# The mLSTM states of a bidirectional mixer block: value index innermost, and one instruction per step in place of scans over time

## The chip, the cores and the metric

The kernel runs on one core of one Trainium2 chip. The time is the device time of one launch in microseconds, the median of several runs. TensorE's clock shows in the profile as a granted share of its full speed.

## What is computed

A backbone of two layers (DEPTH = 2) works on 1280 tokens: 256 context tokens and 1024 latent ones, 1024 features each. A layer normalizes, projects its input into the columns of four mixers (mLSTM, differential attention, gated linear attention GLA, gated DeltaNet), runs the four, and joins them in one output projection with a gated residual. The second layer returns only latent tokens. The change concerns the mLSTM, which runs in both directions over the tokens; the backward direction takes the context tokens from last to first, then the latent ones from last to first.

```python
def _mlstm_run(q, k, v, log_i, log_f, state):
    ...
    def step(carry, inp):
        C, n, m = carry
        ...
        num = (w_inter[..., None] * jnp.einsum('bhtd,bhde->bhte', qc, C)
               + jnp.einsum('bhts,bhse->bhte', s, vc))
        nq = w_inter * jnp.einsum('bhtd,bhd->bht', qc, n) + jnp.sum(s, axis=-1)
        h = num / jnp.maximum(jnp.abs(nq), jnp.exp(-m_t))[..., None]
        ...
        C = w_c[..., None, None] * C + jnp.einsum('bhs,bhsd,bhse->bhde', w_s, kc, vc)
        n = w_c[..., None] * n + jnp.einsum('bhs,bhsd->bhd', w_s, kc)
        return (C, n, m_new), h
    state, h = lax.scan(step, state, tuple(_to_chunks(a) for a in (q, k, v, log_i, log_f)))
```

The memory C (64 by 64 for each of four heads) and its normalizer n (64) thus follow a recurrence over chunks of tokens: the new one is the old one times a decay, plus the chunk's own product of keys and values. The kernel keeps n as a 65th column of C.

## The kernel before

**Tiles and names.** The 1280 tokens are NT = 10 tiles of 128 (2 context, 8 latent), and a tile is the mLSTM's chunk. The states lie in two tiles of on-chip memory, cs0 (forward, d = 0) and cs1 (backward, d = 1). Axis 0 of cs holds two heads (x) of 64 key features each, axis 1 the pair of heads (hp), then come 130 values (2 times 65; of these, 65 belong to each x) and innermost the 10 places in the order of the direction (p). Two values that are neighbours in one state therefore lie ten elements apart. wdec holds the decay of each tile, direction and head, one number for each of the 128 lanes.

**The state part** (`mlstm`, before the mark "mlstm.out") goes through all ten tiles in both layers. `state_in` loads the tile's keys (kq, three buffers) and values (mv), TensorE transposes the keys into a PSUM tile m, an evacuation (`evac`, a copy that goes to ScalarE or VectorE) brings them to a buffer named pd (three buffers), and GpSimd weighs the values beside them. `state_out` forms the products of keys and weighed values in another PSUM tile m and copies them to cs at place p, 64 lanes by 130 values at a time: four copies a tile, two for each direction, none for a direction's last tile. After the ten tiles come eight scans over time (the instruction TENSOR_TENSOR_SCAN, 64 lanes by 65 values by 10 places), each of which turns the products of one head and direction into states. A scan needs a tile of decays as large as its own operand. It is built in a pd buffer by two GpSimd memsets and by copies from wdec, four times a layer.

**The output part** (`first`, `second`, `post`, `norms`) goes over the layer's output tiles, ten in layer 0 and eight in layer 1. `load` fetches for each tile a pd buffer with a broadcast of rs_NG (128 by 1024, 0.52 MB), kq (128 by 1024), mv, and two wb; GpSimd and ScalarE form the weights, TensorE multiplies (pp from kq; m from cs and wb, which is where cs is read; m from mv and pd), VectorE normalizes, and SyncE writes the tile's result from hy to y in the chip's memory. pd, kq and wb have three buffers each, so a tile's load waits until the tile three before it is done.

**What runs beside it.** `out_first` takes the output product of the other three mixers' finished features (k = 2, 3, 6, 7) tile by tile: y is loaded and turned (tr, yT), TensorE forms o, VectorE multiplies by the gate (o from o and gtb) and adds the residual (st from o and st), and SyncE writes st to xp in the chip's memory and loads the next residual into st (two buffers). Only when this is through for all tiles ("out first") can `outproj` begin, which does the remaining k (0, 1, 4, 5): it loads y, x from xp and the gate gtb, turns, multiplies, and adds. In layer 1 GLA's results are also still being written (y from hy, four transfers at a time, and gz loads).

**What sets the order.** Each part is a strand with a rank. A scheduler that runs when the kernel is built takes instructions from the strands by estimated clocks of the engines and puts each at the end of its engine's queue. All instructions go through one helper line, L406, so the profile's rows are told apart by the names of tiles. An engine's queue is worked off in order. SyncE's (SP) holds nearly all transfers: if one waits for its data or its buffer, all behind it wait too. A change of one strand's instructions moves those of every strand behind it.

Of the kernel before, what the change touches and what calls it, by code (L numbers as in the profile page):

```python
# [17 lines left out]
ALU = mybir.AluOpType  # L18
# [8 lines left out]
NT = T // 128  # L27
NCT = NCTX // 128
# [8 lines left out]
ORDER = (tuple(range(NT)), tuple(range(NCT - 1, -1, -1)) + tuple(range(NT - 1, NCT - 1, -1)))  # L37
# [392 lines left out]
def _build(tc, nc, A, out, root, dbg):  # L430
    q_ = Issue()
    q_.log = dbg.get("log")
    V, S, G, P = (Eng(q_, e, r) for e, r in zip("VSGP", (nc.vector, nc.scalar, nc.gpsimd, nc.tensor)))
# [1425 lines left out]
    def mlstm_open(L, st):  # L1859
        M = Box()  # L1860
        M.p = p = Pool(st, "ml")
        M.ps = Pool(st, "mlps", PSUM)

        M.cs = [p([128, 2, 130, NT], f"cs{d}") for d in range(2)]

        M.vt = [p([128, 4, 65], f"mv{i}") for i in range(3)]
        M.wdec = p([128, 2, 2, NT], "wdec")
        return M

    def mlstm(L, M):  # L1870
        l = L.l
        mp_, pps, cs, wdec = M.p, M.ps, M.cs, M.wdec
# [40 lines left out]
        def state_out(t, kt, vws):  # L1913
            pu = pps([128, 2, 2, 65], "m", 2)
            for d, vw in vws.items():
                for h in range(4):
                    hp, x = divmod(h, 2)
                    P.matmul(pu[64 * x:64 * x + 64, d, hp, :], kt[:, 64 * h:64 * h + 64], vw[:, h, :],
                             start=True, stop=True, tile_position=(0, 64 * x))
            for d in vws:  # L1920
                p = ORDER[d].index(t)
                for x in range(2):
                    xs = slice(64 * x, 64 * x + 64)
                    evac(cs[d][xs, :, 65 * x:65 * x + 65, p], pu[xs, d])
        prev = None
        for t in range(NT):
            cur = state_in(t)
# [1 line left out]
                state_out(*prev)  # L1929
            prev = cur  # L1930
        state_out(*prev)
        for d in range(2):
            for hp in range(2):
                dec = mp_([128, 1024], "pd", 3)[:, :650].rearrange("p (a b) -> p a b", b=NT)
                if d == 0:
                    sl = [(wdec[:, 0, hp, 1:NT - 1], 1, NT - 1)]
                else:
                    sl = [(wdec[:, 1, hp, 0:1], 1, 2), (wdec[:, 1, hp, NT - 1:NCT:-1], 2, NT - 1)]

                G.memset(dec[:, :, 0:1], 0.0)  # L1940
                G.memset(dec[:, :, NT - 1:NT], 0.0)
                for (src, a, b) in sl:
                    V.tensor_copy(dec[:, :, a:b], src.unsqueeze(1).to_broadcast([128, 65, b - a]))
                for x in range(2):
                    xs = slice(64 * x, 64 * x + 64)
                    c_ = cs[d][xs, hp, 65 * x:65 * x + 65, :].rearrange("p a b -> p (a b)")
                    V.tensor_tensor_scan(c_, dec[xs].rearrange("p a b -> p (a b)"), c_, 0.0, ALU.mult, ALU.add)
        mark(f"{l}mlstm.out")
        for b in ("mo", "mz"):
            q_.need((l, b))  # L1950
# [38 lines left out]
        def post(i):  # L1989
            b = lds[i]  # L1990
            t = b.t
# [4 lines left out]
            for d in range(2):  # L1996
                p = ORDER[d].index(t)
                nv = pps([128, 4, 65], "m", 2)
                nvs.append(nv)
                if p > 0:  # L2000
                    for hp in range(2):
                        P.matmul(nv[:, 2 * hp:2 * hp + 2, :].rearrange("p a b -> p (a b)"), b.wb[:, d, hp, :], cs[d][:, hp, :, p - 1],
                                 start=(hp == 0), stop=False)
                for h in range(4):
                    P.matmul(nv[:, h, :], b.pd[:, d, h, :], b.vt[:, h, :], start=(p == 0), stop=(p == 0 or h == 3))
# [935 lines left out]
```

## Time and profile before

| | |
|---|---|
| median of 3 runs | 2445.36 us (2436.24 to 2446.64) |
| the profiled execution | 2444.86 us |
| its span, first to last instruction | 2443.0 us |
| mean granted TensorE clock | 0.937 |
| TensorE busy | 2141.1 us, 88% of the span |
| VectorE busy | 1513.1 us, 62% |
| ScalarE busy | 987.4 us, 40% |
| GpSimd busy | 850.4 us, 35% |
| DMA | 335.37 MB, mean 137 GB/s |

Read the shares as averages over a launch whose parts have different limits. Layer 0's state part and output part of the mLSTM lie between about 1045 and 1250 us of the span, layer 1's between about 2190 and 2396 us. PE is TensorE's multiplications, PEld its weight loads, DVE is VectorE, ACT ScalarE, POOL GpSimd, SP SyncE; an arrow reads output, then input.

### The profile page before, as it was taken

How to read it: one execution, taken by the hardware profiler on the slowest of the kernel's cores; microseconds unless marked ns; L12 is line 12 of the kernel's file. 1: busy time of each engine (PE TensorE's matmuls, PEld its weight loads, DVE VectorE, ACT ScalarE, POOL GpSimd, SP SyncE). 2: the span in 40 equal slices, each digit the busy share in tenths (PEclk: the TensorE clock that was granted, in tenths of full speed). 3: DMA queues.
4: the chain of work that ended last, by engine and by line, in shares of the span. 5: the costliest groups of instructions: out<-in, count | busy, mean ns of one | idle time of the engine just before them, and what ended most of it. 6: DMA issues, size and time to landing. Idle time of an engine off the chain costs nothing.

```text
span 2443.0 us, 57689 instructions
## 1 busy us (share of the span) xinstructions
PE 2141.1 (88%) x23367; PEld 1762.3 (72%) x23367; DVE 1513.1 (62%) x2676; ACT 987.4 (40%) x2169; POOL 850.4 (35%) x1075
## 2 busy tenths in 40 slices
PE   5899999999898998886868798889999989977888
PEld 1656778888776687865756677888888667866776
DVE  3586679555386854546556396686642778555665
ACT  2346412333376853222424255412322677533240
POOL 1343523554122225241522163623442122254340
PEclk8899999999999999988989899999999999976989
DMA  7347643455513134157953135432444331353694
GB/s 260 116 133 228 198 140 109 138 152 157 143 46 91 51 84 147 51 143 213 279 178 133 43 124 173 158 113 93 148 149 126 91 100 38 75 152 85 186 277 172
DMA packets 348051, 335.37 MB, mean 137 GB/s; under 512 B 93146, under 2 KB 292282, under 8 KB 347274
## 3 DMA queue, kind: packets, MB, share of 16 engines
q1 hardware_dynamic: 347786, 331.69, 45.6%
q8 instruction: 185, 3.03, 0.5%
q14 instruction: 80, 0.66, 0.1%
HBM read 226.78 MB, written 107.43 MB: 137 GB/s over the span
## 4 chain that ended last, share of the span: by engine, by line
PE 55%; DMA 13%; DVE 11%; issue 8%; ACT 6%; SPq 5%; POOL 2%; ACTq 0%; POOLq 0%; DVEq 0%
PE mm L406 26%; PE po L406 5%; SPq L406 5%; PE tr L406 4%; PE o L406 4%; PE sc L406 3%; PE p L406 3%; PE pd L406 3%; DVE st L406 2%; DMA wm<-in_w_mod 2%; PE puw L406 2%; ACT p L406 2%; PE m L406 2%; DVE cacc L406 1%; DMA KT<-akh 1%
## 5 line engine op out<-in xcount | busy, mean ns | idle before, releaser
L406 PE MATMUL mm<-w,hT 128*128 128x256 f32 x4512 | 645.6, 294 | 20.7 <-DVE st L406 10.0
L406 PEld LDWEIGHTS mm<-w,hT 128*128 128x128 f32 x4512 | 580.9, 195 | 52.9 <-issue 20.4
L406 PE MATMUL mm<-hT,w 128*128 128x512 f32 (+1 forms) x1680 | 388.9, 377 | 19.0 <-DVE w L406 4.9
L406 PEld LDWEIGHTS mm<-hT,w 128*128 128x128 f32 x1680 | 283.1, 195 | 90.0 <-issue 19.6
L406 DVE TENSOR_REDUCE st<-sc 128x1 f32<-128x1024 f32 (+1 forms) x200 | 200.2, 1027 | 69.8 <-PE sc L406 68.3
L406 ACT ACTIVATE p<-sc,st 128x256 f32<-128x256 f32 (+1 forms) x272 | 211.3, 786 | 68.8 <-DVE st L406 54.8
L406 POOL TENSOR_TENSOR w<-wr,w 128x512 fp32r<-128x512 f32 x62 | 87.4, 1411 | 235.5 <-ACT w L406 199.4
L406 POOL TENSOR_TENSOR hss<-hss,mhalf 128x2 f32<-128x2 f32 (+2 forms) x72 | 105.7, 1467 | 181.7 <-DVE hss L406 175.8
L406 PE MATMUL o<-wo,yT 128*128 128x512 f32 x540 | 155.2, 425 | 8.6 <-DVE x L406 7.1
L406 PE MATMUL sc<-KT,qt 96*128 96x512 f32 (+1 forms) x400 | 124.9, 402 | 30.3 <-DMA KT<-akh 13.3
L406 POOL TENSOR_TENSOR ss<-ss,mhalf 128x1 f32<-128x1 f32 (+1 forms) x39 | 68.2, 1749 | 193.4 <-DVE ss L406 185.4
L406 PEld LDWEIGHTS o<-wo,yT 128*128 128x128 f32 x540 | 105.7, 202 | 34.7 <-issue 5.6
L406 ACT COPY st<-mm 128x512 f32<-128x512 f32 (+1 forms) x83 | 45.8, 552 | 202.0 <-PE mm L406 140.9
L406 ACT COPY wt<-tr 128x512 f32<-128x512 f32 (+1 forms) x200 | 102.2, 511 | 60.4 <-PE tr L406 59.8
L406 PE MATMUL o<-w,yT 128*128 128x512 f32 x324 | 107.3, 462 | 21.8 <-DVE st L406 12.3
L406 PE MATMUL tr<-k_ident,p 128*128 128x128 f32 x656 | 114.7, 280 | 7.5 <-ACT wt L406 7.2
L406 POOL TENSOR_TENSOR st<-st 128x1 f32<-128x1 f32 (+1 forms) x136 | 26.6, 195 | 266.5 <-ACT p L406 196.9
L406 ACT CAST w<-wr 128x512 fp32r<-128x512 f32 x128 | 76.8, 620 | 103.7 <-PE mm L406 52.6
L406 PEld LDWEIGHTS sc<-KT,qt 96*128 96x128 f32 x400 | 63.8, 197 | 60.4 <-ACT p L406 32.0
L406 PE MATMUL po<-wt,av 128*64 128x128 f32 x1312 | 103.0, 282 | 2.0 <-DVE aacc L406 2.0
L406 DVE SCALAR_TENSOR_TENSOR p<-p,st,p 128x1280 f32<-128x1280 f32 (+1 forms) x72 | 103.0, 1431 | 2.6 <-POOL st L406 2.5
L406 DVE TENSOR_TENSOR w<-wr,w 128x512 fp32r<-128x512 f32 x66 | 59.1, 895 | 68.6 <-ACT w L406 64.9
(315 smaller groups left out, 4125.8 us busy)
## 6 DMA issues: line engine op xcount, KB each, us to landing
wr<-in_w_in SPq DMA_DIRECT2D x64, 512.0 KB
wm<-in_w_mod SPq DMA_DIRECT2D x64, 256.0 KB
y<-y SPq DMA_DIRECT2D x36, 256.0 KB
xp<-st SPq DMA_DIRECT2D x18, 512.0 KB
pd<-rs_NG SPq DMA_DIRECT2D x18, 512.0 KB
kq<-kq SPq DMA_DIRECT2D x18, 512.0 KB
x<-xp SPq DMA_DIRECT2D x18, 512.0 KB
wm<-in_w_mod SPq DMA_DIRECT2D x16, 512.0 KB
```

What stands on the lines that cost most here:

```text
L406: r = fn(*a, **k)
```

## The change

cs is laid out with the value index innermost, so that one state of one pair of heads is 130 neighbouring elements. The scans go, and with them the memsets and copies that built the decays in pd buffers. For the forward direction each tile's state is made in `state_out` itself: four VectorE instructions a tile (64 lanes by 65 values; tiles after the first) take the previous state, multiply it by the decay, one number per lane, and add the product straight from PSUM; these replace two copies. For the backward direction the copies stay, and after all tiles 16 VectorE instructions a layer (128 lanes by 130 values) go from state to state in the backward order. The multiplication that reads cs now reads neighbouring elements.

```diff
-        M.cs = [p([128, 2, 130, NT], f"cs{d}") for d in range(2)]
+        M.cs = [p([128, 2, NT, 130], f"cs{d}") for d in range(2)]
...
-                    xs = slice(64 * x, 64 * x + 64)
-                    evac(cs[d][xs, :, 65 * x:65 * x + 65, p], pu[xs, d])
+                    xs, es = slice(64 * x, 64 * x + 64), slice(65 * x, 65 * x + 65)
+                    if d == 1 or p == 0:
+                        evac(cs[d][xs, :, p, es], pu[xs, d])
+                    else:
+                        for hp in range(2):
+                            V.scalar_tensor_tensor(cs[d][xs, hp, p, es], cs[d][xs, hp, p - 1, es], wdec[xs, d, hp, t:t + 1],
+                                                   pu[xs, d, hp, :], ALU.mult, ALU.add)
...
-        for d in range(2):
+
+        for p in range(1, NT - 1):
+            t = ORDER[1][p]
             for hp in range(2):
-                dec = mp_([128, 1024], "pd", 3)[:, :650].rearrange("p (a b) -> p a b", b=NT)
-                if d == 0:
-                    sl = [(wdec[:, 0, hp, 1:NT - 1], 1, NT - 1)]
-                else:
-                    sl = [(wdec[:, 1, hp, 0:1], 1, 2), (wdec[:, 1, hp, NT - 1:NCT:-1], 2, NT - 1)]
-
-                G.memset(dec[:, :, 0:1], 0.0)
-                G.memset(dec[:, :, NT - 1:NT], 0.0)
-                for (src, a, b) in sl:
-                    V.tensor_copy(dec[:, :, a:b], src.unsqueeze(1).to_broadcast([128, 65, b - a]))
-                for x in range(2):
-                    xs = slice(64 * x, 64 * x + 64)
-                    c_ = cs[d][xs, hp, 65 * x:65 * x + 65, :].rearrange("p a b -> p (a b)")
-                    V.tensor_tensor_scan(c_, dec[xs].rearrange("p a b -> p (a b)"), c_, 0.0, ALU.mult, ALU.add)
+                V.scalar_tensor_tensor(cs[1][:, hp, p, :], cs[1][:, hp, p - 1, :], wdec[:, 1, hp, t:t + 1], cs[1][:, hp, p, :],
+                                       ALU.mult, ALU.add)
...
-                        P.matmul(nv[:, 2 * hp:2 * hp + 2, :].rearrange("p a b -> p (a b)"), b.wb[:, d, hp, :], cs[d][:, hp, :, p - 1],
+                        P.matmul(nv[:, 2 * hp:2 * hp + 2, :].rearrange("p a b -> p (a b)"), b.wb[:, d, hp, :], cs[d][:, hp, p - 1, :],
```

The scheduler then places all later instructions anew. Three places show it. Numbers behind a name are buffers.

**First place, the end of layer 0's state part.** This is VectorE's queue of the kernel before, from the first tile of decays (pd_13801) to the sum whose result st_13602 SyncE then writes to xp; cs_2116 is forward, cs_2117 backward, and the scans print as SCALAR_TENSOR_TENSOR of 64x650 from pd and cs.

```order
L406 COPY pd_13801<-wdec_12923 128x65x8
L406 SCALAR_TENSOR_TENSOR cs_2116_12918<-pd_13801,cs_2116_12918 64x650 x2
L406 SCALAR_TENSOR_TENSOR wo_2237_13758<-wr_13753,wcol_13580,wo_2235_13756 128x512
L406 COPY pd_13823<-wdec_12923 128x65x8
L406 TENSOR_TENSOR yT_2244_13817<-tr_13818,yT_2243_13816 128x512
L406 SCALAR_TENSOR_TENSOR cs_2116_12918<-pd_13823,cs_2116_12918 64x650
L406 TENSOR_TENSOR o_13764<-o_13764,gtb_13653 128x512
L406 SCALAR_TENSOR_TENSOR cs_2116_12918<-pd_13823,cs_2116_12918 64x650
L406 SCALAR_TENSOR_TENSOR wo_2250_13839<-wr_13835,wcol_13580,wo_2248_13837 128x512
L406 COPY pd_13853<-wdec_12923 128x65
L406 COPY pd_13853<-wdec_12923 128x65x7
L406 TENSOR_TENSOR st_13602<-o_13764,st_13602 128x512
```

The four forward scans stand ahead of that sum; the four backward ones follow behind it, among further sums of `out_first`.

The same place on VectorE's queue in the changed kernel, from the copy of tile 9's transposed keys (pd_13766) on:

```order
L406 COPY pd_13766<-m_13763 128x256
L406 SCALAR_TENSOR_TENSOR wo_2229_13728<-wr_13724,wcol_13570,wo_2227_13726 128x512
L406 SCALAR_TENSOR_TENSOR wo_2230_13729<-wr_13724,wcol_13570,wo_2228_13727 128x512
L406 SCALAR_TENSOR_TENSOR cs_2116_12918<-cs_2116_12918,wdec_12923,m_13774 64x65 x4
L406 TENSOR_TENSOR o_13735<-o_13735,gtb_13639 128x512
L406 TENSOR_TENSOR st_13582<-o_13735,st_13582 128x512
L406 SCALAR_TENSOR_TENSOR cs_2116_12918<-cs_2116_12918,wdec_12923,m_13815 64x65 x4
L406 COPY cs_2117_12919<-m_13815 64x2x65 x2
L406 TENSOR_TENSOR yT_2246_13811<-tr_13812,yT_2245_13810 128x512
L406 SCALAR_TENSOR_TENSOR wo_2239_13789<-wr_13785,wcol_13570,wo_2237_13787 128x512
L406 SCALAR_TENSOR_TENSOR cs_2117_12919<-cs_2117_12919,wdec_12923 128x130 x15
L406 SCALAR_TENSOR_TENSOR wo_2240_13790<-wr_13785,wcol_13570,wo_2238_13788 128x512
```

No scan stands here any more: four forward steps follow each tile's products, and the sum st_13582 of `out_first` stands between tile 8's and tile 9's. The backward steps follow as one row of 15 and one of 1.

SyncE's queue of the kernel before at this place, from the last tile's keys (kq_13698) to the first load of the output part (pd_13894):

```order
L406 DMA kq_13698<-kq_43_120 128x2x128
L406 DMA mv_2118_12920<-mv_71_148 128x4x64
L406 DMA wr_13703<-in_w_out 128x1024
L406 DMA xp_47_124<-st_13320 128x1024
L406 DMA wr_13753<-in_w_out 128x1024
L406 DMA st_13744<-in_x 128x1024
L406 DMA y_13814<-y_31_108 128x2x256
L406 DMA wr_13835<-in_w_out 128x1024
L406 DMA xp_47_124<-st_13602 128x1024
L406 DMA st_13864<-in_x 128x1024
L406 DMA y_13888<-y_31_108 128x2x256
L406 DMA pd_13894<-rs_NG_196 128x8x128
```

The last keys stand ahead of the write of st_13320 to xp, and the first output load stands behind the write of st_13602.

SyncE's queue of the changed kernel, between the same two:

```order
L406 DMA xp_47_124<-st_13320 128x1024
L406 DMA wr_13724<-in_w_out 128x1024
L406 DMA st_13715<-in_x 128x1024
L406 DMA kq_13760<-kq_43_120 128x2x128
L406 DMA mv_2118_12920<-mv_71_148 128x4x64
L406 DMA wr_13785<-in_w_out 128x1024
L406 DMA y_13808<-y_31_108 128x2x256
L406 DMA xp_47_124<-st_13582 128x1024
L406 DMA st_13834<-in_x 128x1024
L406 DMA pd_13893<-rs_NG_196 128x8x128
```

The last keys (kq_13760) now stand behind the write of st_13320 and a load of st; the first output load (pd_13893) still stands behind the second write, now of st_13582.

**Second place, the end of layer 0's output part.** This is SyncE's queue of the kernel before, from the write of the last of the mLSTM's results (hy_14753) to the first loads for `outproj` (y, x, gtb); wr and kq_44 belong to the next layer's projection.

```order
L406 DMA y_31_108<-hy_14753 128x256
L406 DMA wr_14774<-in_w_in 128x4x256
L406 DMA wr_14779<-in_w_in 128x4x256
L406 DMA kq_44_121<-in_k_zero 64x2x1280
L406 DMA y_14785<-y_31_108 128x2x256
L406 DMA x_14786<-xp_47_124 128x1024
L406 DMA kq_44_121<-in_k_zero 64x2x1280
L406 DMA wr_14825<-in_w_in 128x4x256
L406 DMA wr_14827<-in_w_in 128x4x256
L406 DMA y_14848<-y_31_108 128x2x256
L406 DMA x_14849<-xp_47_124 128x1024
L406 DMA gtb_14855<-gt_19_96 128x1024
```

The write of the last result (hy_14753) stands first, and x and gtb, on which `outproj`'s first sums wait, behind it.

The changed kernel's SyncE queue at this place, with hy_14814 the last result:

```order
L406 DMA y_31_108<-hy_14640 128x256
L406 DMA oz_14657<-oz_45_122 128x512
L406 DMA y_14663<-y_31_108 128x2x256
L406 DMA x_14664<-xp_47_124 128x1024
L406 DMA y_31_108<-hy_14724 128x256
L406 DMA oz_14746<-oz_45_122 128x512
L406 DMA x_14770<-xp_47_124 128x1024
L406 DMA gtb_14772<-gt_19_96 128x1024
L406 DMA y_31_108<-hy_14776 128x256
L406 DMA y_14804<-y_31_108 128x2x256
L406 DMA y_31_108<-hy_14814 128x256
```

The first y and x for `outproj` stand ahead of the last three results, the second x and gtb ahead of the last two.

**Third place, the start of layer 1's output part.** This is SyncE's queue of the kernel before; the transfers y from hy in groups of four and the gz loads are GLA's, and pd_27093 is the first load of the mLSTM's output part.

```order
L406 DMA xp_48_125<-st_26313 128x1024
L406 DMA st_26828<-x_26_103 128x1024
L406 DMA y_27020<-y_32_109 128x2x256
L406 DMA y_32_109<-hy_26938 32x8x64 x4
L406 DMA gz_27041<-gz_90_167 32x8x64 x4
L406 DMA xp_48_125<-st_26519 128x1024
L406 DMA y_27087<-y_32_109 128x2x256
L406 DMA pd_27093<-rs_NG_206 128x8x128
L406 DMA kq_27096<-kq_44_121 128x8x128
L406 DMA mv_4110_25326<-mv_72_149 128x4x64
L406 DMA wb_27099<-rs_WI_207 64x4x128 x2
L406 DMA oz_27094<-oz_46_123 128x512
```

Three writes to xp and a group of GLA's writes stand here, the first pd load behind them all.

The changed kernel's SyncE queue at this place:

```order
L406 DMA xp_48_125<-st_26338 128x1024
L406 DMA pd_26955<-rs_NG_206 128x8x128
L406 DMA kq_26958<-kq_44_121 128x8x128
L406 DMA mv_4097_25245<-mv_72_149 128x4x64
L406 DMA wb_26961<-rs_WI_207 64x4x128 x2
L406 DMA oz_26956<-oz_46_123 128x512
L406 DMA oz_26972<-oz_46_123 128x512
L406 DMA st_26913<-x_26_103 128x1024
L406 DMA y_32_109<-hy_26965 32x8x64 x4
L406 DMA gz_27015<-gz_90_167 32x8x64 x4
L406 DMA pd_27058<-rs_NG_206 128x8x128
```

The first pd load stands right behind the write of st_26338, which answers to st_26313 of before, and the second (pd_27058) behind the next group of GLA's writes; later writes to xp stand behind both.

## Rows read from the trace of the kernel before

**Rows 1.** page, section 1: busy time of each engine, share of the span, instructions

```profile
PE 2141.1 (88%) x23367; PEld 1762.3 (72%) x23367; DVE 1513.1 (62%) x2676; ACT 987.4 (40%) x2169; POOL 850.4 (35%) x1075
```

**Rows 2.** windows of layer 0: stretch, its us, busy (x) of PE PEld DVE ACT POOL, PEclk, DMA share, GB/s

```profile
1070.00:1090.00 20.00, 19.73 (x382) 15.68 (x381) 6.14 (x12) 4.21 (x10) 7.03 (x9) 0.87 0.53 143
...
1130.00:1150.00 20.00, 12.98 (x44) 10.01 (x45) 15.95 (x22) 3.04 (x9) 1.97 (x3) 0.67 0.68 199
...
1150.00:1170.00 20.00, 17.00 (x93) 14.38 (x91) 8.96 (x21) 7.03 (x26) 7.80 (x11) 0.91 1.09 273
...
1170.00:1200.00 30.00, 26.67 (x148) 24.23 (x148) 18.95 (x42) 11.71 (x41) 15.40 (x21) 0.89 1.07 282
```

**Rows 3.** timeline of VectorE, layer 0: start us, us, operation

```profile
1123.91 3.03 DVE L406 TENSOR_TENSOR_SCAN cs<-pd,cs 64x650 f32<-64x650 f32 x2
...
1133.31 0.68 DVE L406 TENSOR_TENSOR st<-o,st 128x512 f32<-128x512 f32 x1
...
1138.62 3.01 DVE L406 TENSOR_TENSOR_SCAN cs<-pd,cs 64x650 f32<-64x650 f32 x2
```

**Rows 4.** SyncE's DMA issues, layer 0, same columns: start us, us, transfer

```profile
1106.36 0.55 SPq L406 DMA_DIRECT2D kq<-kq  x1
...
1113.69 0.33 SPq L406 DMA_DIRECT2D xp<-st  x1
...
1118.51 0.33 SPq L406 DMA_DIRECT2D st<-in_x  x1
...
1134.01 0.33 SPq L406 DMA_DIRECT2D xp<-st  x1
...
1137.60 0.59 SPq L406 DMA_DIRECT2D pd<-rs_NG  x1
```

**Rows 5.** timeline of TensorE, layer 0

```profile
1110.15 0.66 PE L406 MATMUL m<-k_ident,kq 128*128 128x128 f32 x2 [3.65 <-DMA kq<-kq]
```

**Rows 6.** tile cs, whole span: count, duration ns min/median/max, first and last start us

```profile
L406 PE MATMUL m<-cs,wb x136: 389/412/586, 1151.8 to 2388.0; 128*128 128x130 f32 x136
...
L406 DVE COPY cs<-m x32: 375/392/410, 1078.9 to 2279.8; 64x130 f32<-64x130 f32 x32
...
L406 DVE TENSOR_TENSOR_SCAN cs<-pd,cs x16: 1491/1506/1818, 1123.9 to 2301.8; 64x650 f32<-64x650 f32 x16
```

**Rows 7.** tile wdec on VectorE, same columns

```profile
L406 DVE COPY pd<-wdec x12: 214/394/439, 1123.4 to 2296.9; 128x520 f32<-128x520 f32 x4, 128x65 f32<-128x65 f32 x4, 128x455 f32<-128x455 f32 x4
```

**Rows 8.** tile S, the state of another mixer, same columns

```profile
L406 DVE SCALAR_TENSOR_TENSOR S<-S,egb,p x160: 161/276/283, 468.7 to 1878.6; 128x64 f32<-128x64 f32 x160
```

**Rows 9.** VectorE's groups by form: count, busy us, mean ns, idle before

```profile
L406 DVE SCALAR_TENSOR_TENSOR oz<-oz 128x256 f32<-128x256 f32 x18 | 8.9, 492 | 0.0
```

**Rows 10.** tile pp, TensorE

```profile
L406 PE MATMUL pp<-kq x144: 270/275/552, 1148.1 to 2384.6; 128*128 128x128 f32 x144
```

**Rows 11.** SyncE's DMA issues at the end of layer 0

```profile
1240.08 0.32 SPq L406 DMA_DIRECT2D y<-hy  x1
...
1242.98 0.62 SPq L406 DMA_DIRECT2D x<-xp  x1
```

**Rows 12.** timeline of VectorE, after the end of layer 0's mLSTM

```profile
1258.17 0.70 DVE L406 TENSOR_TENSOR o<-o,gtb 128x512 f32<-128x512 f32 x1
```

**Rows 13.** SyncE's DMA issues, layer 1

```profile
2281.00 0.54 SPq L406 DMA_DIRECT2D xp<-st  x1
...
2298.01 0.34 SPq L406 DMA_DIRECT2D xp<-st  x1
...
2299.07 0.63 SPq L406 DMA_DIRECT2D pd<-rs_NG  x1
...
2304.79 2.32 SPq L406 DMA_DIRECT2D y<-hy  x4
...
2308.65 0.37 SPq L406 DMA_DIRECT2D pd<-rs_NG  x1
...
2315.17 0.42 SPq L406 DMA_DIRECT2D pd<-rs_NG  x1
```

## The prediction

> **What bounds the kernel now.** I read the shares first. TensorE is busy 88% of the span and VectorE 62% [rows 1], so over the whole launch a change on VectorE should be worth little. Then I cut the region of layer 0's mLSTM into stretches [rows 2]. In the state part TensorE is busy 19.73 of 20 us and VectorE 6.14. Where the scans stand, from 1130 to 1150, it is the other way round: VectorE 15.95 of 20, TensorE 12.98 at a granted clock of 0.67. In the output part transfers rise to 273 and 282 GB/s, and TensorE is at 17.00 of 20 and 26.67 of 30. So only the hole between the two parts has VectorE for its bound.
>
> The timeline of VectorE shows the hole: the first pair of scans starts at 1123.91, the last pair at 1138.62 and takes 3.01 [rows 3]. The sums of the output product that runs beside it stand between the scans: one at 1133.31 takes 0.68, and the write to xp that it releases is issued at 1134.01 [rows 3, 4]. SyncE's queue shows what hangs on that: the first load of the output part, pd at 1137.60, stands right behind this write [rows 4]. The output part starts late because its loads queue behind a write whose sum queues behind scans.
>
> **The cost of the instructions.** Removed are 16 scans at 1.506 us, 24.1 us in both layers, and 12 copies of decays at 0.394, 4.7 [rows 6, 7]. Of the 72 copies of products, 32 went to VectorE at 0.392 [rows 6]; the forward direction loses 32 copies in all, so VectorE loses about 14, 5.6 us. Added are 32 forward steps a layer (8 tiles, 4 each) and 16 backward steps. The forward step is the operation of the tile S with one lane-wise factor: 0.276 us at 64 elements [rows 8]. Before shows no such step that reads PSUM, and none of 130 elements. With one operand in PSUM I bound it by 0.276 and by 0.392, a whole copy of 130 elements from PSUM [rows 6] (7.4 us more over 64 steps), and take the lower, which is the same operation at the same width. For 130 I interpolate between 0.276 at 64 and 0.492 at 256 [rows 8, 9] and get 0.35. The sum is 64 x 0.276 + 32 x 0.35 = 28.9 us added against 34.4 removed: VectorE's busy time hardly changes. What changes is where it stands.
>
> [...]
>
> **Forward steps: covered.** A tile's four steps take 1.1 us, where a copy or so on VectorE (0.39) went before. In the state part VectorE stands idle 13.9 of 20 us under TensorE's 19.73 [rows 2], and that work hides them. If the cover is gone they cost 1.1 − 0.39 = 0.7 for each of 16 tiles, 11.5 us.
>
> **Layer 0, start of the output part: −7.** The block from 1123.91 to 1138.62 + 3.01, 17.7 us with sums in between, gives way to 16 backward steps, 5.6 us. I follow the changed queue (first place). The last keys stand behind the write to xp and the load of st, which before were issued at 1113.69 and 1118.51, so at about 1118.9 and not at 1106.36 [rows 4]. Keys reach TensorE 3.8 us after issue, 1106.36 to 1110.15 [rows 4, 5]: 1122.7. Then VectorE does, in the order shown, a copy (0.4), two weight pieces and two sums of 512 elements (4 x 0.68 = 2.7) and one forward group (1.1): the write goes at 1126.9. From write to first load it took 1137.60 − 1134.01 = 3.6 [rows 4]: 1130.5 instead of 1137.60, −7.1. The bounds are 0, if the output part's own transfers limit it anyway, and the block's shrinkage, 17.7 − 5.6 = 12.
>
> **Layer 0, end of the output part: −12.** Before, the last result is written at 1240.08, the loads for the output product follow (x at 1242.98), and its first sum on VectorE runs at 1258.17: 18.1 us [rows 11, 12]. In the changed queue (second place) y, x, x and gtb stand ahead of the last two results. They move 0.26 + 3 x 0.52 = 1.83 MB, and at the 282 GB/s of [rows 2] that is 6.5 us that the mLSTM's own loads now share. I take 18.1 − 6.5 = 11.6 as gain. The bounds are 0 and 18.1.
>
> **Layer 1, start of the output part: −4.** The third place shows the first pd load right behind the write that stood at 2281.00 instead of behind the one at 2298.01: 2299.07 becomes about 2282, up to −17. The second load then stands behind the group of GLA's writes of before the second xp, the third behind that of 2304.79 with 2.32 for its issue, so at about 2307 instead of 2315.17 [rows 13]: the gain shrinks from −17 over some −13 to −8. Three buffers hold three tiles, so the later loads follow the third; between −8 and −13 I take −9. One more turn of the other product (y, st and xp, 1.3 MB, 4.6 us at 282 GB/s) then falls into the output part: −9 + 4.6 = −4.4. The bounds are 0 and −17.
>
> **Multiplications with cs: 0.** They take 0.412 us with elements ten apart; those of pp, of 128 neighbouring columns, 0.275 [rows 6, 10]. 136 x 0.137 = 18.6 us of TensorE's time may go, all in output parts where it is busy 85 to 89% and waits for loads [rows 2]; the cover is the loads, and without it the 18.6 us would count in full. GpSimd's memsets of decays go too; it is busy 1.97 of 20 us there [rows 2].
>
> The sum: −7.1 − 11.6 − 4.4 = −23.1 on the profiled execution's 2444.86 us (span 2443.0, the rest around it), 0.5 us under the median. Forecast: **2422 us**. A measurement tells about 0.5%, 12.2 us, from no change, so faster begins at 2433.
>
> **The rivals.**
> First, the head start is not kept at the end of layer 0: the projection's weights and the output product's loads wait for transfers of the mLSTM at 282 GB/s, and the hole of 18.1 us only moves. For it: the output part has the highest DMA rate [rows 2]; against: 1.83 MB is small. −7.1 − 4.4 gives 2433.
>
> Second, the small steps are on the path after all. Each tile's state waits for the last one, and VectorE's queue is in order; products of the next tile need the two PSUM buffers m, which the steps hold longer than copies did. For it: by 1130 to 1150 VectorE is the busy engine; against: 6.14 of 20 in the state part [rows 2]. +11.5 gives 2433. [...]
>
> Third, no gain that shows: the loads of pd wait for buffers and for the other product's transfers wherever they stand, and all starts shift without the ends. 2440 to 2447, say 2444.
>
> Fourth, slower: a ring between VectorE and SyncE. A forward group stands at the head of VectorE's queue and waits for keys whose load stands behind a write to xp that VectorE's next sum must release. Each such turn costs 4.8 (write to next load of st, 1113.69 to 1118.51), 3.8 for the keys, and 0.4 + 1.1 on VectorE, 10.1, where the write alone takes 4.8: 5.3 us more [rows 4, 5, 6]. It eats the forecast from five turns on (23.1/5.3 = 4.4); with eight of the 16 tiles it is +42 − 23 = +19, 2464. For it: one such turn shows in the changed queue (first place); against: only one there, and in layer 1 the last keys stand ahead of the writes.
>
> Fifth, TensorE was the bound in the output parts, and the 18.6 us count: 2422 − 18.6 = 2403. For it: 88% busy [rows 1]. If the multiplication stays at 0.412 with neighbouring elements, so that this part of the change does nothing, my sum is untouched.
>
> **How the numbers follow.** Forecast 0.55, first rival 0.15, second 0.10, third 0.08, fourth 0.07, fifth 0.05. The forecast's own range, with one of the three terms at a bound, is 2405 to 2433. For 8 in 10 the range must reach to the fifth rival and the third: 2403 to 2442, which leaves out the slower case and part of the tails. Faster: 0.55 + 0.05 + half of the first two rivals (they lie on the boundary), 0.72; same: the other half and the third, 0.21; slower: 0.07.
>
> **What would show it.** Right: no scans; steps near 0.28 and 0.35 us; the first pd load some 7 us earlier after the last keys in layer 0; under 10 us between the last result and the first sum of the output product; in layer 1 the first pd load within 2 us of an xp write. Wrong: a wait of VectorE on products of TensorE with an xp write behind it in several tiles; DMA over 282 GB/s with pd loads taking longer than before; steps over 0.5 us; an unchanged distance from the first pd load to the last result. The forecast falls most easily through the 11.6, which rests on an order and on one rate.

## The result and the profile after

The changed kernel takes 2416.79 us, median of 4 runs (2405.2 to 2417.39), against 2444.89 for the kernel before: a ratio of 0.9876, 95% interval 0.9851 to 0.9902. Measured once more on another occasion (first experiment), it was 2420.82 against 2440.09, 0.9911 (0.9886 to 0.9937). The gain is 28 us the first time and 19 the second; about 23 were forecast.

The profiled execution of the changed kernel, 2405.2 us, is the fastest of its four. It is 39.7 us under that of the kernel before, more than the medians differ, so the two traces must be compared stretch by stretch. The page's busy line, beside [rows 1]:

```profile
PE 2113.9 (88%) x23367; PEld 1737.7 (72%) x23367; DVE 1500.8 (62%) x2726; ACT 981.6 (41%) x2168; POOL 834.4 (35%) x1048
```

The shares hardly move: TensorE stays at 88%, VectorE loses 12 of 1513 us. What the instructions cost shows in the view of tile cs (count, duration min/median/max, first and last start):

```profile
L406 PE MATMUL m<-cs,wb x136: 272/275/557, 1132.8 to 2343.9; 128*128 128x130 f32 x136
L406 DVE SCALAR_TENSOR_TENSOR cs<-cs,wdec,m x64: 246/282/293, 1076.9 to 2248.4; 64x65 f32<-64x65 f32 x64
L406 ACT COPY cs<-m x34: 251/263/265, 1070.1 to 2252.0; 64x130 f32<-64x130 f32 x34
L406 DVE SCALAR_TENSOR_TENSOR cs<-cs,wdec x32: 340/349/354, 1117.7 to 2256.4; 128x130 f32<-128x130 f32 x32
L406 DVE COPY cs<-m x6: 284/296/297, 1070.7 to 1116.1; 64x130 f32<-64x130 f32 x6
L406 POOL MEMSET cs<- x4: 2255/2260/2262, 1039.0 to 2156.5; 128x2600 f32 x4
```

The scans are gone, a forward step takes 0.282 us, a backward one 0.349. Against [rows 6], the multiplications fall from 0.412 to 0.275 and the copies that stay on VectorE from 0.392 to 0.296.

The last row also says where layer 0's mLSTM begins, with the first clearing of cs: at 1039.0, and at 1045.5 before. Up to there the two programs are the same, so these 6.5 us belong to the execution. Over the 14 profiles of this study that clearing starts between 1038.3 and 1049.0. From it on I measure with landmarks that every trace has: the first load of pd, the write of the mLSTM's last result, the last sum of layer 0's output product, the end. SyncE's issues in front of the first load, beside [rows 4] (start us, us, transfer):

```profile
1103.41 0.33 SPq L406 DMA_DIRECT2D xp<-st  x1
...
1106.39 0.33 SPq L406 DMA_DIRECT2D st<-in_x  x1
1106.82 0.39 SPq L406 DMA_DIRECT2D kq<-kq  x1
...
1114.84 0.33 SPq L406 DMA_DIRECT2D xp<-st  x1
1117.46 0.33 SPq L406 DMA_DIRECT2D st<-in_x  x1
1117.90 0.37 SPq L406 DMA_DIRECT2D pd<-rs_NG  x1
```

From the clearing to the first pd load it is 78.9 us, where it was 1137.60 − 1045.5 = 92.1. The keys stand behind the write at 1103.41 and the load of st, as the order said. But the sum that releases the next write did not wait for them. TensorE turns the keys of one tile in each such row; these are the last two:

```profile
1108.94 0.38 PE L406 MATMUL m<-k_ident,kq 128*128 128x128 f32 x2
1111.88 0.38 PE L406 MATMUL m<-k_ident,kq 128*128 128x128 f32 x2
```

VectorE, then ScalarE:

```profile
1110.72 0.41 DVE L406 COPY pd<-m 128x256 f32<-128x256 f32 x1
...
1114.12 0.69 DVE L406 TENSOR_TENSOR st<-o,st 128x512 f32<-128x512 f32 x1
```

```profile
1114.01 0.37 ACT L406 COPY pd<-m 128x256 f32<-128x256 f32 x1
```

Tile 9's keys are turned at 1111.88, 5.1 us after their load was issued, and copied by ScalarE at 1114.01. VectorE's copy at 1110.72 runs ahead of both: it is tile 8's. So pd_13766 of the first place holds tile 8's keys and not tile 9's, and the forward steps shown there are those of tiles 7 and 8 (tile 9, the last of the forward direction, has none). VectorE is busy without a break from 1107.13 to the end of the sum that starts at 1114.12; that work, not the last keys, lies ahead of the write at 1114.84.

At the end of the output part, beside [rows 11, 12], first SyncE, then VectorE:

```profile
1204.03 1.62 SPq L406 DMA_DIRECT2D x<-xp  x1
...
1210.84 0.44 SPq L406 DMA_DIRECT2D x<-xp  x1
1211.33 0.42 SPq L406 DMA_DIRECT2D gtb<-gt  x1
...
1219.30 0.32 SPq L406 DMA_DIRECT2D y<-hy  x1
```

```profile
1218.38 0.68 DVE L406 TENSOR_TENSOR x<-o,x 128x512 f32<-128x512 f32 x1
```

The output product's first sum into x ends before the last result is even written. From that write to the start of the sum it is −0.9 us, where it was 18.8 (1240.08 to 1258.9). The stretches, in us, worked out from the starts of the same landmarks in each trace:

| | clearing to first pd load | to last result | to last sum of layer 0 | layer 0, sum | from there to the end |
|---|---|---|---|---|---|
| before | 92.1 | 102.5 | 107.4 | 302.1 | 1095.5 |
| changed | 78.9 | 101.4 | 91.7 | 272.0 | 1092.3 |
| changed, again | 81.1 | 105.3 | 91.7 | 278.2 | 1093.5 |

Layer 0 gains 24 to 30 us, 11 to 13 at the start and 15.7 at the end of the output part; all of the rest of the launch 2 to 3.

### The profile page after: what moved, and what is told of

Same layout as the page of the kernel before. It is cut to its first block, busy times and chain, and to the rows that moved or that the text cites. A ratio compares the mean times of both kernels' runs of the same rounds, so it can differ in the third digit from the quotient of the medians.

```text
span 2403.3 us, 57716 instructions
## 1 busy us (share of the span) xinstructions
PE 2113.9 (88%) x23367; PEld 1737.7 (72%) x23367; DVE 1500.8 (62%) x2726; ACT 981.6 (41%) x2168; POOL 834.4 (35%) x1048
## 5 line engine op out<-in xcount | busy, mean ns | idle before, releaser
L406 DVE TENSOR_REDUCE st<-sc 128x1 f32<-128x1024 f32 (+1 forms) x200 | 200.0, 1026 | 66.8 <-PE sc L406 65.6
L406 POOL TENSOR_TENSOR w<-wr,w 128x512 fp32r<-128x512 f32 x54 | 80.7, 1495 | 275.3 <-ACT w L406 220.9
L406 PE MATMUL o<-wo,yT 128*128 128x512 f32 x540 | 148.9, 412 | 4.8 <-DVE x L406 3.2
L406 ACT COPY wt<-tr 128x512 f32<-128x512 f32 (+1 forms) x200 | 102.2, 511 | 66.0 <-PE tr L406 65.6
L406 PE MATMUL po<-wt,av 128*64 128x128 f32 x1312 | 105.3, 284 | 3.5 <-DVE aacc L406 3.5
L406 PE MATMUL o<-w,yT 128*128 128x512 f32 x324 | 100.9, 439 | 4.0 <-DVE st L406 4.0
L406 DVE TENSOR_TENSOR w<-wr,w 128x512 fp32r<-128x512 f32 x74 | 68.1, 922 | 54.5 <-ACT w L406 54.3
```

The source lines that it names most:

```text
L406: r = fn(*a, **k)
```

## The experiments

Ratios are to the kernel before, run beside each. The changed kernel's own time stood beside the first four only (2420.82 us); the kernel before had 2440.09 us beside these and 2442.48 and 2442.92 beside the later ones, so a difference of a later run to the changed kernel is good to some 3 us. Each kernel has one profile; its stretches:

| kernel | time, us | ratio (95%) | to first pd load | to last result | to last sum | layer 0 | to the end |
|---|---|---|---|---|---|---|---|
| strided | 2420.77 | 0.9922 (0.9894 to 0.9949) | 83.6 | 102.4 | 92.2 | 278.2 | 1096.1 |
| layer 0 alone | 2417.64 | 0.9901 (0.9877 to 0.9924) | 82.8 | 100.7 | 92.1 | 275.6 | 1099.0 |
| layer 1 alone | 2451.28 | 1.0043 (1.0026 to 1.0060) | 91.5 | 104.2 | 109.1 | 304.8 | 1096.6 |
| start-up held back | 2443.65 | 1.0004 (0.9985 to 1.0023) | 81.2 | 101.5 | 109.7 | 292.4 | 1109.4 |
| first load held back | 2437.34 | 0.9979 (0.9962 to 0.9996) | 87.8 | 106.5 | 84.3 | 278.7 | 1117.4 |
| before, scans swapped | 2460.22 | 1.0080 (1.0052 to 1.0108) | 90.4 | 105.7 | 109.7 | 305.8 | 1112.0 |
| block | 2440.28 | 0.9985 (0.9963 to 1.0007) | 80.8 | 110.9 | 91.1 | 282.9 | 1110.3 |
| block, prefetch | 2439.64 | 0.9991 (0.9976 to 1.0006) | 83.6 | 108.1 | 93.3 | 285.0 | 1112.6 |
| prefetch | 2437.35 | 0.9971 (0.9956 to 0.9986) | 73.8 | 110.8 | 96.3 | 280.9 | 1112.4 |
| late steps | 2435.74 | 0.9979 (0.9959 to 1.0000) | 74.5 | 106.8 | 110.2 | 291.5 | 1096.9 |
| reversed | 2416.40 | 0.9893 (0.9869 to 0.9916) | 81.7 | 101.9 | 91.0 | 274.7 | 1096.2 |

**The changed kernel again.** No edit.

> The changed kernel once more. Against the profiled execution of the kernel before, that of the changed kernel is 6 us ahead where the state part of layer 0 begins, in front of anything that the change moves, gains 29 us more in layer 0, gives back 11 between 1400 and 1900 us in layer 1 (same work, TensorE's granted clock 0.92 to 0.93 in stretches that had 0.97 and more), and gains 14 at the end of layer 1. Theory: the 29, the 11 and the 14 belong to the order of the instructions and come again within 3 us each; the 6 belongs to the execution and does not. Rival: the 11 is the execution's own too, and a second profile shows less than 5 given back. Time 2405 to 2418 either way.

Measured 2420.82 us (0.9911), above the range. The execution's own 6 us turn to 3.5 behind, as the theory said. Layer 0 gains 24, not 29 within 3: an execution moves this stretch by 6 us too. The "11 given back" was a reading that did not last, though it came again in size: it compared equal instructions of strands that the new order interleaves differently. At 2000 to 2050 us of the kernel before, attention's products (po from wt and av) run 25.6 us earlier in the changed kernel and the projection's (mm from w and hT) 57. From layer 0's last sum to the end the whole stretch is 2 us shorter, not longer.

**Old layout, new instructions.**

```diff
-        M.cs = [p([128, 2, NT, 130], f"cs{d}") for d in range(2)]
+        M.cs = [p([128, 2, 130, NT], f"cs{d}") for d in range(2)]
...
-            if f == 4 and step > 1 and n > 32:
+            if f == 4 and step > 1 and step != NT and n > 32:
```

The accesses to cs follow the layout; the second edit keeps the scheduler's estimate, and so the order, as it was.

> The changed kernel with the old layout: values ten elements apart, the same instructions in the same order on every engine. Theory (the gain is transfers that start earlier; multiplications with cs hide behind loads): time within 0.3% of the changed kernel, 2412 to 2424, although 136 multiplications go back from 275 to about 412 ns and the steps may lengthen by some tens of ns. Rival (the neighbouring operand makes the gain): 18.6 us slower than the changed kernel or more, 2435 to 2442.

```profile
L406 PE MATMUL m<-cs,wb x136: 389/412/528, 1138.7 to 2354.6; 128*128 128x130 f32 x136
L406 DVE SCALAR_TENSOR_TENSOR cs<-cs,wdec,m x64: 296/332/353, 1077.2 to 2256.8; 64x65 f32<-64x65 f32 x64
L406 ACT COPY cs<-m x34: 380/387/407, 1070.2 to 2260.5; 64x130 f32<-64x130 f32 x34
L406 DVE SCALAR_TENSOR_TENSOR cs<-cs,wdec x32: 440/458/499, 1120.5 to 2266.3; 128x130 f32<-128x130 f32 x32
```

Every instruction on cs is slower again, the multiplications by 137 ns each (0.275 to 0.412 us), and the time is 2420.77 against 2420.82. The layout buys 18.6 us of TensorE's busy time and nothing of the launch's that shows: each ratio is known to about 0.003, some 7 us. Why elements ten apart take longer, no run shows.

**One layer alone.** In the other layer layout, copies and scans stay.

```diff
+        if l in (0,):
...
```

> The change in layer 0 alone; layer 1 keeps layout, copies and scans. The order is that of the changed kernel up to layer 1's state part. Theory: -29 in layer 0 and +11 in layer 1's projection, so -18: 2424 to 2430. Rival (layer 0's head start is lost wholly by the end of layer 1): 2440 or more. Rival (the 11 is chance): -25 or more, below 2420.

> The change in layer 1 alone; the order is that of the kernel before up to layer 1's state part. Theory from the traces: -14 at the end of layer 1, 2428 to 2434. Prediction's term: -4.4, about 2440. Rival (gains of the two layers come only together): no change, 2444.

Layer 0 alone gives the whole gain (0.9901): 2417.64 us, which is the case of the rival that took the 11 for chance. Layer 1 alone makes the kernel slower by 0.43%, which no expectation had; its profile, 2446.43 us, is one of its shorter executions and shows 1.6 us of it. SyncE's queue in layer 1 has there

```profile
2275.49 3.17 SPq L406 DMA_DIRECT2D y<-hy  x4
2278.70 1.96 SPq L406 DMA_DIRECT2D gz<-gz  x4
2280.76 0.40 SPq L406 DMA_DIRECT2D kq<-kq  x1
```

The last keys wait behind GLA's four writes. From the clearing of cs to the last tile's transposes it takes 96.9 us, where before took 79.5 and the changed kernel 86.7 and 87.5. So "−14 at the end of layer 1" was not layer 1's edit: from layer 1's clearing to the end the kernel with layer 0 alone, without that edit, takes 253.4 us, the changed one 249.1 and 251.4, before 256.2, and this one, with the edit, 257.3.

**Start-up of the output product held back (layer 0).**

```diff
             q_.need((l, "out first"))
+            if l == 0:
+                q_.need((l, "mlstm", len(L.yt) - 1))
```

> The changed kernel, but in layer 0 the output product may start its loads only when the mLSTM's last result is made, as it stood before the change. All instructions up to the loads of the last mLSTM tiles keep the changed kernel's order. In the traces the distance from the last result's write to the output product's first sum went from +18.8 us to -0.9, of which its own length gave back 4. Theory (this is the larger half of layer 0's gain): +15 against the changed kernel, 2431 to 2438. Prediction's first rival (the hole only moves, because transfers bound it): less than +5, under 2426.

```profile
1221.52 5.47 SPq L406 DMA_DIRECT2D y<-hy  x2
1227.05 0.56 SPq L406 DMA_DIRECT2D y<-y  x1
...
1230.21 0.60 SPq L406 DMA_DIRECT2D y<-y  x1
1230.86 0.78 SPq L406 DMA_DIRECT2D x<-xp  x1
```

The loads follow the last results again, and the stretch to the last sum is 109.7 us: the 15.7 of the end come back as 18.0, and the start keeps its 11. Layer 0 loses 14 to 20, as the theory says. But the time loses 23, above both ranges, because what follows takes 1109.4 us in place of 1092 to 1094, in a part whose code was not touched. The first rival is out; the size of the total is not the theory's.

**First load held back (layer 0).**

```diff
+                if l == 0 and i == 0:
+                    q_.need((l, "first", 4))
                 lds[i] = load(i)
```

> The changed kernel, but in layer 0 the first load of the mLSTM's output part waits until the other product's fifth tile is written, one write to xp later than in the changed kernel, so some 10 us later. Nothing is removed or added. Theory (the output part starts when its first load can start, and its length is its own): +8 to +11, 2427 to 2432. Rival (the start of this part is hidden, and only the order of the output product counts): within 4 us of the changed kernel, 2417 to 2425.

The first load comes 7 to 9 us later, as set. Layer 0 still takes 278.7: the mLSTM's last result is late, but the output product by then runs (its first sum comes 19.9 us ahead of that result) and fills the time. So within layer 0 the rival holds. The time is 17 us longer than the changed kernel's all the same, above both ranges, again in what follows: 1117.4 us.

**Before, with the backward scans first.**

```diff
-        for d in range(2):
+        for d in (1, 0):
             for hp in range(2):
                 dec = mp_([128, 1024], "pd", 3)...
```

> The kernel before, with the backward scans ahead of the forward ones: the same work, another order from there on. Theory (the gain has its cause in the change, not in any shift of the order): within 0.4% of the kernel before, 2431 to 2450. Rival (a new order alone is worth some 1%): outside that, faster or slower.

The rival's case: the same work in another order is 0.8% slower, 3.7 us of it in layer 0 and 16.5 behind it.

**A block of VectorE work where the scans stood (layer 0).**

```diff
+        if l == 0:
+            for d in range(2):
+                for hp in range(2):
+                    c_ = cs[d][:, hp, 0:NT - 1, :].rearrange("p a b -> p (a b)")
+                    for x in range(2):
+                        V.scalar_tensor_tensor(c_, c_, 1.0, c_, ALU.mult, ALU.max)
```

> The changed kernel with eight more VectorE instructions in layer 0 where the scans stood: each multiplies 128 x 1170 state values by 1.0 in place, an estimated 1.3 to 1.4 us from the 512-element steps (0.75) and the copies, some 11 us in all, which leaves the states as they are. Theory (the block of VectorE work behind the state part holds up the sums of the other product and the output part): +7 to +13, 2427 to 2434. Rival (the block is no matter, since its sums wait for transfers anyway, and the gain is one of the queue's order): under +4, 2417 to 2424.

```profile
L406 DVE SCALAR_TENSOR_TENSOR cs<-cs x8: 1365/1368/1370, 1130.6 to 1142.6; 128x1170 f32<-128x1170 f32 x8
```

10.9 us of work cost layer 0 5 to 11 us, close to what the theory had, all in the output part (110.9 in place of 101 to 105). The scheduler put the block behind the first pd load, which is issued at 1126.51, so this run does not tell what such a block costs ahead of it, where the forward scans stood. The time loses 20, more than either expectation. In layer 1, SyncE's queue has

```profile
2275.51 1.83 SPq L406 DMA_DIRECT2D y<-hy  x4
2277.43 3.07 SPq L406 DMA_DIRECT2D gz<-gz  x4
2280.55 0.45 SPq L406 DMA_DIRECT2D kq<-kq  x1
...
2284.28 0.33 SPq L406 DMA_DIRECT2D st<-x  x1
2284.65 0.43 SPq L406 DMA_DIRECT2D kq<-kq  x1
```

with two loads of keys behind writes, and the state part there takes 114.5 us.

**The same block, keys of layer 1 loaded two tiles ahead.** In `state_in`:

```diff
-            if t + 1 < NT:
+            if l == 1:
+                for j in ((1, 2) if t == 0 else (t + 2,)):
+                    if j < NT:
+                        kvs[j] = load_kv(j, j)
+            elif t + 1 < NT:
                 kvs[t + 1] = load_kv(t + 1, t + 1)
```

> The kernel with eight more VectorE instructions in layer 0, and in layer 1 the mLSTM's keys are loaded two tiles ahead in place of one. In the run with the eight instructions alone, layer 0 lost 5 to 11 us against the changed kernel, and layer 1's state part took 114.5 us from the clearing of cs to the last tile's transposes, where the changed kernel took 86.7 and 87.5; there two loads of keys stand behind writes of the other product and of GLA. Theory (those two loads are what layer 1 lost, about 17 us of the end): the state part takes under 95 us, one load of keys at most stands behind a write, and the time is 2420 to 2431. Rival (the state part is longer for another reason): still over 105 us, 2436 to 2444.

The state part falls to 104.7 us and the time stays (2439.64): from layer 0's last sum to the end 1112.6 us. My theory that the late keys are what layer 1 loses falls; 104.7 lies between it and the rival.

A state part of 104.7 or 114.5 us should not be set against the changed kernel's 87 either. In both block kernels, and with the start-up held back (114.6), 1155 to 1174 of GLA's products (pd from qm and km) run behind the clearing of cs in layer 1, where the changed kernel has 790: the clearing itself stands earlier in the order, and the stretch holds more of other strands' work.

**Keys two tiles ahead in both layers of the changed kernel.** The same edit with the condition true.

> The changed kernel with keys loaded two tiles ahead in both layers. In layer 0 the first load of the output part then stands behind one write to xp less. Theory (queue positions in front of the output part carry the gain): layer 0's first output load some 5 us earlier, time 2408 to 2421, equal to the changed kernel or up to 10 us faster. Rival (layer 0's output part is bound by its transfers, an earlier load changes nothing; or the new order costs elsewhere): 2417 to 2435.

The first load comes 5 to 7 us earlier, at 73.8, and the output part is longer by 5.5 to 9.4 (110.8). Layer 0 gains nothing, what follows takes 1112.4, and the time, 2437.35, lies above both ranges.

**Forward steps after all tiles.** All products are copied, then 32 steps a layer of 128 x 130.

```diff
-                    if d == 1 or p == 0:
-                        evac(cs[d][xs, :, p, es], pu[xs, d])
-                    else:
...
+                    evac(cs[d][xs, :, p, es], pu[xs, d])
...
-        for p in range(1, NT - 1):
-            t = ORDER[1][p]
+        for d in range(2):
+            for p in range(1, NT - 1):
+                t = ORDER[d][p]
```

> The new layout and single instructions, but the forward steps come after all tiles like the backward ones: 32 instructions of 128 x 130 a layer in one block (11.2 us in place of 5.6), and copies for all products. VectorE's total work is about that of the changed kernel. Theory (the block behind the state part costs its length): +5 to +8 in layer 0, 2424 to 2430, and layer 1 as the order falls. Rival (any single-instruction form does, since only the scans' copies, memsets and buffers mattered): within 3 us of the changed kernel. Rival (block of 11 us acts as the eight extra instructions did): 2436 or more.

No expectation is met as it was reasoned: the first load stands at 74.5 us, earliest but one, yet layer 0 takes 291.5, because the start-up hole is back:

```profile
1219.01 0.32 SPq L406 DMA_DIRECT2D xp<-st  x1
...
1222.29 0.32 SPq L406 DMA_DIRECT2D y<-hy  x1
...
1225.84 0.64 SPq L406 DMA_DIRECT2D x<-xp  x1
```

The other product's last write goes at 1219.01, 3.3 us ahead of the mLSTM's last result; before they were 4.7 apart, in the changed kernel 26.5 (1192.8 to 1219.30).

**Backward copies ahead of forward steps.**

```diff
-            for d in vws:
+            for d in reversed(list(vws)):
                 p = ORDER[d].index(t)
```

> The changed kernel with each tile's backward copies placed ahead of its forward steps: the same work. The order of layer 0 is nearly that of the changed kernel, and in layer 1 one load of keys falls behind a write to xp. Theory: layer 0 as in the changed kernel (272 to 278 us from the clearing of cs to the last sum of the output product); layer 1 loses some 5 to 15 us by that load: 2422 to 2432. Rival (such a load costs nothing): within 4 us of the changed kernel, 2416 to 2424.

Layer 0 is as in the changed kernel, 274.7. In layer 1 the load behind a write does lengthen the state part to 96.9 us, but from there to the end it is 7 to 9 shorter, and the time is the changed kernel's (2416.40). The rival was right: in this order such a load costs the launch nothing that shows.

## Why the prediction held, point by point

**Durations.** Right: 0.282 for 0.276, 0.349 for 0.35. But the kernel before does have such a step that reads PSUM: p of [rows 8], which TensorE writes, lies there, so the 0.276 held that operand already, and what it costs no run shows. Missed: the copies that stay are shorter too, VectorE's 0.296 us in place of 0.392 and ScalarE's 0.263 in place of 0.388, with results side by side in place of ten apart, and VectorE's busy time fell by 12.3 us where I had 5.5. Of its copies of products VectorE lost 26 (32 to 6), not 14, as the evacuations fell to the engines anew.

**Forward steps covered.** In layer 0 the state part up to the last tile's transposes grew from 67.5 to 73.0 and 75.2 us, by 5.5 and 7.7. The last keys, behind a write as forecast, account for it: issued 67.8 us after the clearing in place of 60.9 (1106.82 − 1039.0 against 1106.36 − 1045.5). That the steps are covered shows in the prefetch kernel, which has them and its keys early: 65.6 us, less than before. The second rival, 11.5 us for the steps, does not hold in layer 0.

**Start of layer 0's output part, −7.** Mis-sized, 11 to 13, and the chain that gave it did not run. I let the write wait for the last keys, with 3.8 us from their load to TensorE. In the kernel before:

```profile
1104.79 0.38 SPq L406 DMA_DIRECT2D kq<-kq  x1
...
1112.83 0.63 PE L406 MATMUL m<-k_ident,kq 128*128 128x128 f32 x2
```

The row at 1110.15 [rows 5] is tile 8's, whose load was issued at 1104.79; tile 9's load at 1106.36 leads to 1112.83. The times are 5.4 and 6.5 us, and 3.8 joins the load of one tile to the transposes of the one before. In the changed kernel the write did not wait for the last keys at all. That it took 11.1 us from their load to the first pd load, where my chain has 11.6, is chance. What holds is that the first load follows the write and that the write comes earlier without scans: the three kernels with scans in layer 0 have the first load 90.4 to 92.1 us after the clearing, the others 73.8 to 83.6, and 87.8 where it was held back. Some 10 us of layer 0 stay when the start-up hole is back (292.4 and 291.5 in place of 302.1). But the start is no clock that runs one for one. Moved 7 to 9 us late, it made layer 0 longer by 0.5 to 6.7, less than its delay, since the stretch behind the last result got 7 shorter; 5 to 7 us early it gained nothing, since the output part got longer.

**End of layer 0's output part, −12.** The step that carries the result, and mis-sized too: 15.7 net, of which the first sum gained 19.7 and the product's length gave 4.0 back (88.6 to 92.6 from first to last sum), where I had charged 6.5 for transfers. Holding the start-up back and the late steps both show it: with the hole, 109.7 and 110.2 us from the last result to the last sum; in the changed kernel without it 91.7. The first rival is refuted. The cause that I named was the order of loads; what lets them stand there is that the other product is through 26.5 us before the mLSTM. Taking the scans out does not by itself bring that about: the late steps have none, and there it is 3.3. Why is not shown.

**Start of layer 1's output part, −4.** The size from clearing to end is near (−7.1 and −4.8 in the two profiles), but the cause fails. The first pd load follows the last transposes by 14.2 and 15.1 us in place of 32.8, as the order said, and it stands 0.65 us behind a write to xp in the first of them, but the last transposes come 7 to 8 later. And layer 1's change alone gains nothing, it costs 0.43%, while layer 0's alone gains all. Moving its loads is worth nothing that I could show.

**Multiplications, 0.** Right: the strided kernel shows it, and the fifth rival, 18.6 us more of gain, falls with it: the strided kernel would have been slower by as much. The third, no gain that shows, falls by the result.

**The slower rival** was priced for VectorE and one write that waits for it. The one such turn that I saw in the changed queue is none: the forward group there is tile 7's and needs no late keys. A load of keys behind writes does come about, in layer 1 and behind GLA's writes; one such load was free in one order (reversed), and undoing one of two brought no time.

**What was not in the prediction at all** is the price of a new order further on. From layer 0's last sum to the end, the 14 profiles fall in two groups: 1092.3 to 1099.0 us (eight, that of before among them) and 1109.4 to 1117.4 (six), with the same work or nearly so. Layer 0's gain of 24 to 30 us has the cause of its larger half shown, the start-up; but whether it reaches the end of the launch hangs on the order behind it. With the first load held back, layer 0 still gains 23 us and the launch 5 (2437.34 against 2442.48).

Where the second group loses its time can be read. At layer 1's last product of GLA's from us and gq, counted from layer 0's last sum, the first group stands at 944.1 to 958.6 us, the second at 966.2 to 978.7; behind it they do not differ (137.0 to 151.3 and 132.9 to 145.8). At the first product of layer 1's attention (po from wt and av) it is 584 and 596 on average. So most of the loss lies ahead of layer 1's mLSTM, in strands that no edit touches. What puts an order there stays open. Late keys of the mLSTM do not (reversed has them and is fast). Nor does TensorE's clock part the groups: from layer 0's last sum to layer 1's clearing of cs, 0.94 to 0.96 were granted in all 14 (0.95 in before and in the changed kernel); over the whole launch the profiles of the second group show a little less, 0.929 to 0.936 against 0.935 to 0.942.

**The sum.** The terms measured −11 to −13 and −15.7 in layer 0, where I had −18.7 together, and −2 to −3 for all the rest of the launch, where I had −4.4. Between the landmarks that makes 26 to 33 us of gain (with −1.1 and +2.8 for the output part of layer 0) against 23.1; the two medians, 28 and 19, lie on either side. So the direction and the two places in layer 0 were foreseen. That the number is near is in part luck: the chain behind the first term was misread, and the changed kernel's order happened to fall in the first group. My own range had a slip as well: with one term at a bound it begins at 2409, not 2405.

No version beat the changed kernel: strided, layer 0 alone and the reversed one are within its spread.

## What to carry to other kernels

When a change shortens a block on one engine, look for what stands idle after it and for who finishes last of two strands that a third one waits for: here 15.7 us came from a product that now ends ahead of its neighbour, and nothing that shows from 18.6 us of faster multiplications. Where a scheduler places every instruction anew, run a variant with the same work in another order before the gain is put down to the change; here one such variant moved the time by 0.8%, another by nothing that shows. Before a chain of waits is built on a queue's order, find out which tile each of its instructions serves. And compare traces by stretches between landmarks, with the same work in the stretch: 14 executions differed by 10.7 us ahead of the first instruction that any of these edits changes.

## What the runs showed of the hardware

Elements of cs ten apart took longer than elements side by side on all three engines that were measured, not on TensorE alone: ScalarE's copy of 64 x 130 from PSUM took 0.387 us with results ten elements apart and 0.263 side by side, VectorE's copy 0.390 and 0.296, a step 0.332 and 0.282 at 65 elements, 0.458 and 0.349 at 130, a multiplication 0.412 and 0.275. The first of these I had not expected, since the source, PSUM, was read in the same way in both.
